# Scores of a differential attention: two stacked products over 128 rows, or three over 64

## The chip, the cores and the metric

The kernel runs on one core of a Trainium2 chip. The metric is the device time of one execution in microseconds, as the median of several runs. The engines are named as in the profile: PE is TensorE's matmuls and PEld its weight loads, DVE is VectorE, ACT is ScalarE, POOL is GpSimd, SP is SyncE, which issues most of the transfers. Line numbers such as L921 are those of the kernel before, unless the text says that they are of the kernel after.

## The reference

The reference is one step of a trunk of two layers over 512 sample tokens and 128 prompt tokens with 1024 features. Each layer projects the normalised tokens once, and three branches read the projection: latent attention, differential attention, and a bidirectional mLSTM. Their gated outputs go through one output projection to the residual. The change touches the differential attention. Per head, with `q_b` and `k_b` of 128 features that hold two maps of 64 features each:

```python
o1 = attention(q_b[..., :DIFF_D], keys_b[..., :DIFF_D], vals_b, DIFF_SCALE)
o2 = attention(q_b[..., DIFF_D:], keys_b[..., DIFF_D:], vals_b, DIFF_SCALE)
o_b = rmsnorm(o1 - lam * o2, W['diff_norm'][l]) * (1.0 - lam_init)
```

A sample token attends to the 512 sample keys and to 128 cached context keys, 640 in all; a prompt token attends to the 128 prompt keys.

## The kernel before

All 640 tokens are worked on in five tiles of 128: four of the sample (`t` 0 to 3) and one of the prompt (`t` 4). Large products keep float32 accuracy by splitting each operand in a high part that the fast matmul takes exactly (float32r) and the rest, the low part: `mm3` (L287 to L290) sends high x high, high x low and low x high. Weights stream in sections through `load_w`: a transfer on SP's queue, the high part by ScalarE (L279), the low part by VectorE or GpSimd (L282). Projections of sections are the `tm` (token-major) and `fm` (feature-major) matmuls; `op` is the output projection.

The order of the work is made in two steps. The program text is a chain of dependent steps (four mLSTM heads, four differential heads, then latent attention), each a generator that yields a number of microseconds; at each yield `Feed.pull` (L107) emits that much independent work from a list (`ORDER`, L133), mostly projections. `feed.need` emits at once what a step needs. Then the framework's scheduler, which simulates the engines, orders the instructions of each engine; the queues themselves run in that order.

Differential attention: `sec_dqk` projects q and k of a head, token-major and rotated. `diff_prep` (L882) transposes them into `pq` and `pkd`, feature-major, with map 0 on rows 0 to 63 and map 1 on rows 64 to 127. `q_stack` (L799) then writes for each map one tile `qs` of 128 rows, its high part above its low part. `k_stack` (L808) writes for each map `ksh` (the high part of the keys, twice) and `ksl` (the low part, twice), and the same for the prompt keys in `kp`. So a score needs two products over 128 rows, `[q_hi; q_lo]` with `[k_hi; k_hi]` and with `[k_lo; k_lo]`, and these hold all four partial products:

```python
T.matmul(pv[:, hf], lhsT=lq, rhs=ks[m][0][:, hf * 320:(hf + 1) * 320], start=True, stop=False)
T.matmul(pv[:, hf], lhsT=lq, rhs=ks[m][1][:, hf * 320:(hf + 1) * 320], start=False, stop=True)
```

These are L921 and L922 (L925 and L926 for the prompt tile); `ds` is their tile in PSUM, one of two buffers of two banks that all transposes of a head share with it. `diff_head` (L900) calls `s1(t)` for the scores of a token tile: for each map the matmuls, a reduction to the maximum (L927), a small scaling (L928) and the exponential (L929); then the two maps are combined into one (L932 to L934). `s2_` transposes the result (`pT`), copies it to `PT` and multiplies by the values (`po`). The preparation of head `h + 1` is called in head `h` before the last `s2_`; that of head 0 stands at the start of head 0.

An mLSTM head (`mlstm_head`, L707) works through five token tiles `c`, each ending with L772 to L777 on VectorE, and closes with a norm and `finish`, whose transposes are `oT`.

Of the kernel before, what the change touches and what calls it, by code (L numbers as in the profile page):

```python
# [9 lines left out]
F32 = mybir.dt.float32  # L10
F32R = mybir.dt.float32r
# [7 lines left out]
P = 128  # L19
# [13 lines left out]
# columns of the constant array  # L33
C_ID, C_SEL, C_BLK, C_ONE, C_PRM, C_RC, C_RS, C_MF, C_END = (
    0, 128, 130, 138, 266, 436, 692, 948, 1204)
# columns of the parameters among them
# [29 lines left out]
def parameter_columns(I):  # L66
    """Vectors of the inputs laid out as columns of 128, and the gate biases and stabilisers on their gate rows."""
    names = ("c", "c_ctx", "g_norm", "mla_q_norm", "mla_kv_norm", "diff_norm", "ml_conv", "ml_norm",
             "state_mlstm_n", "b_mod")
    c = np.zeros((P, C_RC - C_PRM), np.float32)  # L70
    c[:, 0:R_GB] = np.concatenate([I[n].reshape(-1, P) for n in names]).T
    for d in range(2):
        for ty in range(2):
            q0 = ty * 64 + d * 32
            c[q0:q0 + H, R_GB:R_GB + DEPTH] = I["ml_gate_b"][:, d, ty, :].T
        c[d * 32:d * 32 + H, R_M0:R_M0 + DEPTH] = I["state_mlstm_m"][0, :, d, :].T
    return c


class Feed:  # L80
    """Independent work, emitted in portions between the steps of a dependent chain."""
# [41 lines left out]
def tile_hybrid(ctx: ExitStack, tc: tile.TileContext, I: dict, O: dict):  # L123
# [8 lines left out]
    # independent work of a layer, in the order in which it fills the gaps of the dependent chains  # L132
# [7 lines left out]
    class Fixed:  # L140
        """One tile from which all that stays in its place is cut."""
# [14 lines left out]
    class Ring:  # L156
        """Slots used in turn, for tiles that live for a short stretch of the program."""
# [32 lines left out]
    # ---------------------------------------------------------------- constants and parameters  # L190
# [12 lines left out]
    # silu(cond) as stationary columns: [c_hi, ctx_hi, c_lo, ctx_lo] per k  # L203
# [13 lines left out]
    # half conv weights; norm gains with the half of z's silu  # L217
# [29 lines left out]
    # ---------------------------------------------------------------- helpers  # L247
    def rsq(ss, n, mul, eps=EPS):
        """1/sqrt(ss*mul + eps) on [P, n] columns."""
# [13 lines left out]
    def load_w(parts, kt, w, pool=3):  # L263
        """Streams a weight section; returns per-k views of its exact high and low parts."""
# [27 lines left out]
    # ---------------------------------------------------------------- modulation  # L292
# [4 lines left out]
    def mod_rows(l, c0, pool):  # L297
        ps = pj("modp")
        if pool is None:
            # before there is other work for the tensor engine: unsplit  # L300
# [34 lines left out]
    def mod_col(l, part, s, res, pool=3):  # L335
        """Columns [P, k, which] of two feature tiles of the shift or of the scale."""
# [13 lines left out]
    def mod_end(l, res, k=slice(0, 8)):  # L350
        """(1 + scale) * g and shift."""
# [21 lines left out]
    def gate_tile(l, hf):  # L373
        """The residual gates of half of the features for the sample and for the prompt, on all partitions."""
# [5 lines left out]
    # ---------------------------------------------------------------- residual stream  # L380
# [48 lines left out]
    def norm_sample(s, xs, mods, hT):  # L429
        """Two feature tiles of the normalised sample: transposed, modulated and split."""  # L430
# [8 lines left out]
    def norm_prompt(s, xs, mods, hT):  # L439
        """Four feature tiles of the normalised prompt."""  # L440
# [16 lines left out]
    # ---------------------------------------------------------------- projections  # L457
# [9 lines left out]
    def fm_unit(hT, wv, c0, cb):  # L467
        """Feature-major unit of 128 columns: cb(half, psum of 320 tokens)."""
# [9 lines left out]
    def tm_unit(hT, wv, w, cb):  # L478
        """Token-major unit: cb(token tile, psum [P, w])."""
# [8 lines left out]
    def z_sec(l, hT, key, c0, res, h):  # L488
        """2 * silu(z) of a head, feature-major."""
# [10 lines left out]
    def head_norm(tok, sq, mul):  # L500
        """rmsnorm over the 128 features of each of the 5 token tiles; in place."""
# [7 lines left out]
    def finish(tok, tmp, gcol, z):  # L509
        """Token-major head output -> gated, feature-major, split in high and low."""  # L510
# [11 lines left out]
    def out_proj(l, br, ks, res, key, v):  # L522
        """x += gate * (heads ks of a branch) @ W_out, for all tokens."""
# [19 lines left out]
    def out_tail(l, br, ks, res, key, v):  # L543
        """The last heads of a layer, token tile by token tile; gives the new residual tiles."""
# [21 lines left out]
    # ---------------------------------------------------------------- branch C: mLSTM  # L566
    def sec_va(l, hT, p, res):
        """Values of a pair of heads (and the gates with the first pair), token-major."""
# [35 lines left out]
    def conv_unit(l, hT, wv, c0, ch, res, key):  # L604
        """Depthwise conv and silu, feature-major."""
# [15 lines left out]
    def gates(l, res):  # L621
# [42 lines left out]
        # final stabilisers of the prompt  # L664
# [42 lines left out]
    def mlstm_head(l, h, res, feed, nfin):  # L707
# [8 lines left out]
        # value of [C | n] at the start of each chunk  # L716
# [33 lines left out]
        for c in range(NT):  # L750
            if c < 4:
                # q scaled by the weight of the incoming state
# [25 lines left out]
            yield 4.8  # L778
        feed.need(("mo", p), ("zc", h))
# [7 lines left out]
    # ---------------------------------------------------------------- attention pieces  # L787
    def rope(dst, x, t, s, on=None):
        """dst, x: [P, s*64] of sample token tile t."""
# [9 lines left out]
    def q_stack(ps, r0, n):  # L799
        """rows r0..r0+64 of ps -> [q_hi; q_lo], for each of r0."""  # L800
# [7 lines left out]
    def k_stack(ps, parts):  # L808
        """(r0, n0, kh, kl): rows r0..r0+64 of ps from column n0 -> [k_hi; k_hi], [k_lo; k_lo]."""
# [11 lines left out]
    def attend(pe, t, v3, vp, hs):  # L821
        """psum [q, dv] = P @ V, P token-major."""
# [12 lines left out]
    # ---------------------------------------------------------------- branch B: differential attention  # L835
    def sec_dv(l, hT, p, res):
        """Values of a pair of heads: sample | context cache, and prompt."""
# [16 lines left out]
    def sec_dqk(l, hT, h, res):  # L854
        """q | k of a head, token-major, rotated; the context cache as fifth key tile."""
# [25 lines left out]

    def diff_prep(l, h, res):  # L882
        x3, pr, kc = res["dqk", h]
# [3 lines left out]
        qs = q_stack(pq, (0, 64), TOK)  # L887
# [5 lines left out]
        kp = qt("kp", F32R, 512)  # L893
        ks = [(qt("ksh", F32R), qt("ksl", F32R)) for m in range(2)]
        kps = [(kp[:, m * 256:m * 256 + P], kp[:, m * 256 + P:m * 256 + 2 * P]) for m in range(2)]
        k_stack(pk, [(64 * m, n0, *k[m]) for n0, k in ((0, ks), (TOK, kps)) for m in range(2)])
        yield 6.4
        res["dst", h] = (qs, ks, kps)

    def diff_head(l, h, res, feed):  # L900
# [9 lines left out]
        def s1(t):  # L910
            sc = st("dsc")
            pe = []
            n = TOK if t < 4 else P
            for m in range(2):
                lq = qs[m][:, t * P:(t + 1) * P]
                ex = qt("P")
                ps = s2("ds")
                if t < 4:
                    pv, ev, ax = halves(ps), ex.rearrange("p (a n) -> p a n", a=2), AX.XY
                    for hf in range(2):  # L920
                        T.matmul(pv[:, hf], lhsT=lq, rhs=ks[m][0][:, hf * 320:(hf + 1) * 320], start=True, stop=False)  # L921
                        T.matmul(pv[:, hf], lhsT=lq, rhs=ks[m][1][:, hf * 320:(hf + 1) * 320], start=False, stop=True)  # L922
                else:
                    pv, ev, ax = ps[:, 0:P], ex[:, 0:P], AX.X
                    T.matmul(pv, lhsT=lq, rhs=kps[m][0], start=True, stop=False)  # L925
                    T.matmul(pv, lhsT=lq, rhs=kps[m][1], start=False, stop=True)  # L926
                V.tensor_reduce(sc[:, m:m + 1], pv, axis=ax, op=ALU.max, negate=True)  # L927
                V.tensor_scalar(sc[:, 2 + m:3 + m], sc[:, m:m + 1], DIFF_SCALE, None, op0=ALU.mult)  # L928
                A.activation(ev, pv, AF.Exp, scale=DIFF_SCALE, bias=sc[:, 2 + m:3 + m], accum_out=sc[:, 4 + m:5 + m])  # L929
                pe.append(ex[:, 0:n])  # L930
                yield 1.5
            V.reciprocal(sc[:, 6:8], sc[:, 4:6])  # L932
# [432 lines left out]
```

## Time and profile before

| | us |
|---|---|
| median of 3 runs | 1401.21 |
| lowest and highest run | 1399.54, 1405.23 |
| span of the profiled execution | 1399.6 |
| matmuls (PE) busy | 1310.0 |
| VectorE busy | 842.5 |
| ScalarE busy | 630.2 |
| GpSimd busy | 385.5 |

The profiled execution's own time is its span, from the first to the last instruction. Busy times overlap: an engine's share of the span says how much room it has, and the waits of the engine that has none say what else the time is made of. A matmul's row has its start and a modelled end; matmuls overlap in the pipeline, so the cost of one is read from the distance between starts. A wait is written behind an instruction as [idle before <- what it waited for].

### The profile page before, as it was taken

How to read it: one execution, taken by the hardware profiler on the slowest of the kernel's cores; microseconds unless marked ns; L12 is line 12 of the kernel's file. 1: busy time of each engine (PE TensorE's matmuls, PEld its weight loads, DVE VectorE, ACT ScalarE, POOL GpSimd, SP SyncE). 2: the span in 40 equal slices, each digit the busy share in tenths (PEclk: the TensorE clock that was granted, in tenths of full speed). 3: DMA queues.
4: the chain of work that ended last, by engine and by line, in shares of the span. 5: the costliest groups of instructions: out<-in, count | busy, mean ns of one | idle time of the engine just before them, and what ended most of it. 6: DMA issues, size and time to landing. Idle time of an engine off the chain costs nothing.

```text
span 1399.6 us, 24039 instructions
## 1 busy us (share of the span) xinstructions
PE 1310.0 (94%) x9300; PEld 1218.9 (87%) x9300; DVE 842.5 (60%) x1786; ACT 630.2 (45%) x1333; POOL 385.5 (28%) x335
## 2 busy tenths in 40 slices
PE   8989999989899999999979899999999999899995
PEld 3789899969899999798769899998799999878984
DVE  2576757765567465854465767675655646385446
ACT  5454544433455545255365345443343445435433
POOL 0421422323223013511432213333322202161142
PEclk9999999999999999999989999999999999999998
DMA  9423323264223223531751333434521211242154
GB/s 341 116 83 101 111 84 112 85 212 136 81 83 111 61 62 113 167 109 54 238 176 31 84 112 86 117 82 129 180 84 57 74 46 63 87 138 85 54 173 150
DMA packets 164642, 156.40 MB, mean 112 GB/s; under 512 B 14193, under 2 KB 130593, under 8 KB 164529
## 3 DMA queue, kind: packets, MB, share of 16 engines
q1 hardware_dynamic: 154032, 135.92, 32.0%
q10 hardware_dynamic: 10496, 18.95, 3.6%
q8 instruction: 73, 1.20, 0.3%
q14 instruction: 41, 0.33, 0.1%
HBM read 131.38 MB, written 23.46 MB: 111 GB/s over the span
## 4 chain that ended last, share of the span: by engine, by line
PE 73%; DVE 12%; DMA 5%; ACT 4%; issue 2%; POOL 2%; SPq 1%; DVEq 0%; ACTq 0%; POOLq 0%
PE tm L288 8%; PE tm L289 8%; PE tm L290 8%; PE fm L288 6%; PE fm L290 6%; PE fm L289 6%; PE po L831 5%; PE op L288 2%; PE pT L826 2%; PE op L289 2%; PE op L290 2%; DVE fixr L282 1%; PE nd L767 1%; PE ds L921 1%; DVE ksl L816 1%
## 5 line engine op out<-in xcount | busy, mean ns | idle before, releaser
L288 PE MATMUL tm<-fixr 128*128 128x256 f32 (+2 forms) x1040 | 302.0, 291 | 12.4 <-DVE kp L816 4.8
L289 PE MATMUL tm<-fixr 128*128 128x256 f32 (+2 forms) x1040 | 299.4, 288 | 0.2 <-DVE fixr L282 0.2
L290 PE MATMUL tm<-fixr 128*128 128x256 f32 (+2 forms) x1040 | 297.0, 287 | 2.5 <-DVE fixr L427 2.2
L282 POOL TENSOR_TENSOR fixr<-fix,fixr 128x1024 fp32r<-128x1024 f32 (+4 forms) x51 | 121.4, 2380 | 385.0 <-ACT fixr L279 365.4
L279 ACT CAST fixr<-fix 128x1024 fp32r<-128x1024 f32 (+2 forms) x154 | 157.8, 1030 | 128.7 <-PE fm L289 38.4
L288 PEld LDWEIGHTS tm<-fixr 128*128 128x128 f32 x1040 | 201.0, 193 | 15.3 <-issue 4.7
L290 PEld LDWEIGHTS tm<-fixr 128*128 128x128 f32 x1040 | 200.3, 193 | 3.0 <-DVE fixr L427 2.4
L289 PEld LDWEIGHTS tm<-fixr 128*128 128x128 f32 x1040 | 201.0, 193 | 1.4 <-issue 0.9
L288 PE MATMUL fm<-fixr 128*128 128x320 f32 x640 | 201.3, 314 | 0.5 <-ACT od L940 0.5
L290 PE MATMUL fm<-fixr 128*128 128x320 f32 x640 | 199.3, 311 | 0.0
L289 PE MATMUL fm<-fixr 128*128 128x320 f32 x640 | 198.6, 310 | 0.0
L282 DVE TENSOR_TENSOR fixr<-fix,fixr 128x1024 fp32r<-128x1024 f32 (+3 forms) x103 | 141.6, 1377 | 66.8 <-ACT fixr L279 62.3
L288 PEld LDWEIGHTS fm<-fixr 128*128 128x128 f32 x640 | 120.3, 188 | 2.2 <-ACT od L940 0.8
L290 PEld LDWEIGHTS fm<-fixr 128*128 128x128 f32 x640 | 120.2, 188 | 0.9 <-issue 0.9
L289 PEld LDWEIGHTS fm<-fixr 128*128 128x128 f32 x640 | 120.4, 188 | 0.0
L539 POOL TENSOR_TENSOR xp<-xp,ytmp 128x512 f32<-128x512 f32 x60 | 79.1, 1329 | 107.7 <-DVE ytmp L538 58.4
L288 PE MATMUL op<-fixr,oTh 128*128 128x512 f32 x240 | 100.5, 419 | 2.9 <-ACT oTh L516 1.7
L289 PE MATMUL op<-fixr,oTh 128*128 128x512 f32 x240 | 96.7, 403 | 0.0
L290 PE MATMUL op<-fixr,oTl 128*128 128x512 f32 x240 | 95.0, 403 | 0.0
L929 ACT ACTIVATE P<-ds,fix 128x640 f32<-128x640 f32 (+1 forms) x80 | 56.7, 709 | 72.7 <-DVE fix L928 70.4
L927 DVE TENSOR_REDUCE fix<-ds 128x1 f32<-128x640 f32 (+1 forms) x80 | 56.8, 713 | 47.4 <-PE ds L922 31.0
L252 POOL TENSOR_TENSOR fix<-fix 128x5 f32<-128x5 f32 (+1 forms) x31 | 31.6, 1019 | 130.4 <-DVE fix L251 129.9
(325 smaller groups left out, 2722.2 us busy)
## 6 DMA issues: line engine op xcount, KB each, us to landing
fix<-in_W_in SPq DMA_DIRECT2D x56, 512.0 KB, 4.2
fix<-in_W_mod SPq DMA_DIRECT2D x35, 512.0 KB, 4.3
fix<-in_W_in SPq DMA_DIRECT2D x64, 256.0 KB, 3.3
xd<-xp ACTq DMA_DIRECT2D x60, 256.0 KB, 2.5
xp<-xd SPq DMA_DIRECT2D x50, 256.0 KB, 4.4
fix<-in_W_out SPq DMA_DIRECT2D x24, 512.0 KB, 5.0
gate<-grow SPq DMA_DIRECT2D x32, 256.0 KB, 5.0
wm<-in_W_mod SPq DMA_DIRECT2D x26, 256.0 KB, 5.9
```

Of the source, the lines that this page charges most:

```text
L252: G.tensor_tensor(r[:, :n], a[:, :n], mhalf[:, :n], op=ALU.pow)
L279: A.copy(hv, rv)
L282: e.tensor_tensor(lv, rv, hv.bitcast(F32), op=ALU.subtract)
L288: T.matmul(ps, lhsT=wh, rhs=xh, start=start, stop=False)
L289: T.matmul(ps, lhsT=wh, rhs=xl, start=False, stop=False)
L290: T.matmul(ps, lhsT=wl, rhs=xh, start=False, stop=stop)
L539: G.tensor_tensor(xt, xt, y, op=ALU.add)
L767: T.matmul(nd[:, d, 0:129], lhsT=e[:, d], rhs=va[:, c, :], start=True, stop=(c == 4))
L826: T.transpose(ps[:, c * P:(c + 1) * P], pe[:, c * P:(c + 1) * P], idt)
L831: T.matmul(po[:, 0:P], lhsT=pt[:, c * P:(c + 1) * P], rhs=v3[:, c] if t < 4 else vp[:, hs], start=(c == 0), stop=(c == n - 1))
L927: V.tensor_reduce(sc[:, m:m + 1], pv, axis=ax, op=ALU.max, negate=True)
L929: A.activation(ev, pv, AF.Exp, scale=DIFF_SCALE, bias=sc[:, 2 + m:3 + m], accum_out=sc[:, 4 + m:5 + m])
```

## The change

Scores are made of three products (high x high, high x low, low x high) over the 64 rows of a map, and the matmuls of the two maps alternate in the program text: map 0 reads rows 0 to 63 and map 1 rows 64 to 127, each into a score buffer of its own. The stacks go: q, k and the prompt's k are split once each on all 128 rows, by `split2`, one ScalarE and one VectorE instruction. The preparation asks for 3.2 instead of 6.4 us of other work at its second pause. The product low x low is no longer computed. Both score buffers and both `P` tiles are taken at the start of `s1`. The preparation of head 0 is called in the last mLSTM head, after its fourth token tile. Comments are dropped too, which moves line numbers only.

```diff
@@ mlstm_head, at the end of the loop over c
             yield 4.8
+            if c == 3 and h == H - 1:
+                feed.need(("dqk", 0))
+                yield from diff_prep(l, 0, res)
@@ before and in diff_prep
+    def split2(hi, lo, src):
+        A.copy(hi, src)
+        V.tensor_tensor(lo, src, hi.bitcast(F32), op=ALU.subtract)
+        return hi, lo
...
-        qs = q_stack(pq, (0, 64), TOK)
+        qs = split2(qt("qh", F32R), qt("ql", F32R), pq[:, 0:TOK])
         yield 2
...
-        kp = qt("kp", F32R, 512)
-        ks = [(qt("ksh", F32R), qt("ksl", F32R)) for m in range(2)]
-        kps = [(kp[:, m * 256:m * 256 + P], kp[:, m * 256 + P:m * 256 + 2 * P]) for m in range(2)]
-        k_stack(pk, [(64 * m, n0, *k[m]) for n0, k in ((0, ks), (TOK, kps)) for m in range(2)])
-        yield 6.4
+        ks = split2(qt("ksh", F32R), qt("ksl", F32R), pk[:, 0:TOK])
+        kp = qt("kp", F32R, 2 * P)
+        kps = split2(kp[:, 0:P], kp[:, P:2 * P], pk[:, TOK:TOK + P])
+        yield 3.2
@@ diff_head, s1(t)
+            kk = ks if t < 4 else kps
+            pss = [s2("ds") for m in range(2)]
+            exs = [qt("P") for m in range(2)]
...
+            for hf, ck in cols:
+                for i_, (a, b) in enumerate(((0, 0), (0, 1), (1, 0))):
+                    for m in range(2):
+                        rows = slice(64 * m, 64 * m + 64)
+                        T.matmul(pvs[m][:, hf], lhsT=qs[a][rows, t * P:(t + 1) * P], rhs=kk[b][rows, ck],
+                                 start=(i_ == 0), stop=(i_ == 2))
             for m in range(2):
...
-                    for hf in range(2):
-                        T.matmul(pv[:, hf], lhsT=lq, rhs=ks[m][0][:, hf * 320:(hf + 1) * 320], start=True, stop=False)
-                        T.matmul(pv[:, hf], lhsT=lq, rhs=ks[m][1][:, hf * 320:(hf + 1) * 320], start=False, stop=True)
...
-                V.tensor_reduce(sc[:, m:m + 1], pv, axis=ax, op=ALU.max, negate=True)
+                V.tensor_reduce(sc[:, m:m + 1], pvs[m], axis=ax, op=ALU.max, negate=True)
```

What the scheduler makes of it, at two places. The first is TensorE's queue in head 0 of layer 0, at one score tile between other matmuls (`op` is the output projection, `tm` a projection of tokens). Before, one map's scores, both column halves:

```order
L290 MATMUL op<-fixr,oTl 128x512
L921 MATMUL ds<-ksh,qs 128x320
L922 MATMUL ds<-ksl,qs 128x320
L921 MATMUL ds<-ksh,qs 128x320
L922 MATMUL ds<-ksl,qs 128x320
L288 MATMUL op<-fixr,oTh 128x512
```

After the change, in the same head (L935 is the line of all score matmuls there):

```order
L289 MATMUL tm<-fixr 128x256
L935 MATMUL ds<-ksh,qh 128x320
L935 MATMUL ds<-ksl,qh 128x320
L935 MATMUL ds<-ksh,ql 128x320
L935 MATMUL ds<-ksh,qh 128x320
L935 MATMUL ds<-ksl,qh 128x320
L935 MATMUL ds<-ksh,ql 128x320
L290 MATMUL tm<-fixr 128x256
```

Again one map stands alone, three products for each of two column halves; the other map's six matmuls stand in another place, with projections between. In the program text the two maps alternate, so that each product would come twice in a row.

The second place is VectorE's queue around the preparation of head 0 in layer 0. Before, it stands behind the finish of the last mLSTM head (L514) and between the output projection's steps (L538), and the first score reductions (L927) follow:

```order
L514 SCALAR_TENSOR_TENSOR sq<-oT,fix,sz 128x640
L347 TENSOR_TENSOR fix<-mcp,fix 128x4
L805 TENSOR_TENSOR qs<-pq,qs 64x640 x2
L538 TENSOR_TENSOR ytmp<-op,gate 128x512
L816 TENSOR_TENSOR ksl<-pkd,ksh 64x640 x4
L816 TENSOR_TENSOR kp<-pkd,kp 64x128 x4
L538 TENSOR_TENSOR ytmp<-op,gate 128x512 x2
L927 TENSOR_REDUCE fix<-ds 128x1 x2
```

After the change:

```order
L282 TENSOR_TENSOR fixr<-fix,fixr 128x1024 x2
L887 TENSOR_TENSOR ql<-pq,qh 128x640
L887 TENSOR_TENSOR ksl<-pkd,ksh 128x640
L347 TENSOR_TENSOR fix<-mcp,fix 128x4
L772 SCALAR_TENSOR_TENSOR fix<-nd,fix 128x2
L773 TENSOR_TENSOR fix<-nd,fix 128x2
L774 RECIPROCAL fix<-fix 128x2
L776 TENSOR_SCALAR hs<-nd,fix 128x128
L887 TENSOR_TENSOR kp<-pkd,kp 128x128
L777 SCALAR_TENSOR_TENSOR hs<-nd,fix,hs 128x128
```

The preparation now stands ahead of the last token tile of the mLSTM head (L772 to L777), in three instructions where there were ten.

## Rows read from the trace of the kernel before

**Rows 1.** The page: busy time of each engine and its share.

```profile
PE 1310.0 (94%) x9300; PEld 1218.9 (87%) x9300; DVE 842.5 (60%) x1786; ACT 630.2 (45%) x1333; POOL 385.5 (28%) x335
```

**Rows 2.** TensorE's waits, 280 to 470 us (layer 0): total us, times, longest.

```profile
PE ds L922 <- DVE ksl L816: 3.9, 1, 3.9
PE tm L288 <- DVE sz L496: 3.0, 1, 3.0
PE ds L921 <- DVE kp L816: 2.3, 1, 2.3
PE tm L288 <- DVE kp L816: 1.5, 1, 1.5
```

**Rows 3.** The same waits from 960 to 1215 us, layer 1.

```profile
PE tm L288 <- DVE kp L816: 3.3, 2, 2.5
PE ds L921 <- DVE kp L816: 2.2, 1, 2.2
PE ds L922 <- DVE ksl L816: 2.0, 1, 2.0
```

**Rows 4.** Windows: length, engines' busy us, then PEclk, DMA share and GB/s.

```profile
280.00:302.00 22.00, 15.78 (x68) 12.63 (x67) 12.43 (x22) 8.61 (x16) 7.76 (x5) 0.84 0.66 215
360.00:376.00 16.00, 11.26 (x67) 10.59 (x66) 11.61 (x18) 6.93 (x14) 3.52 (x2) 0.79 0.44 140
...
974.00:990.00 16.00, 11.76 (x45) 9.21 (x44) 9.59 (x18) 4.85 (x12) 4.22 (x4) 0.79 0.51 164
```

**Rows 5.** Timeline of TensorE, a score tile: first matmul, and the one behind the fourth.

```profile
304.02 0.31 PE L921 MATMUL ds<-ksh,qs 128*128 128x320 f32 x1
...
304.61 0.39 PE L288 MATMUL op<-fixr,oTh 128*128 128x512 f32 x1
```

**Rows 6.** Instructions on the tile `ds`: ns shortest, median, longest; first and last start.

```profile
L921 PE MATMUL ds<-ksh,qs x128: 302/310/605, 288.4 to 1197.5; 128*128 128x320 f32 x128
...
L927 DVE TENSOR_REDUCE fix<-ds x80: 280/815/826, 296.8 to 1207.1; 128x1 f32<-128x640 f32 x64, 128x1 f32<-128x128 f32 x16
L929 ACT ACTIVATE P<-ds,fix x80: 360/794/812, 298.4 to 1207.6; 128x640 f32<-128x640 f32 x64, 128x128 f32<-128x128 f32 x16
```

**Rows 7.** Timeline of TensorE around two matmuls on 4 rows.

```profile
167.08 0.28 PE L288 MATMUL tm<-fixr 128*128 128x256 f32 x1
167.29 0.59 PE L367 MATMUL gtp<-fix 4*2 4x256 f32 x2
167.81 0.39 PE L289 MATMUL tm<-fixr 128*128 128x256 f32 x1
168.03 0.28 PE L290 MATMUL tm<-fixr 128*128 128x256 f32 x1
```

**Rows 8.** Instructions on the tile `gtp`, as in rows 6.

```profile
L367 PE MATMUL gtp<-fix x16: 372/373/374, 136.1 to 949.1; 4*2 4x256 f32 x16
```

**Rows 9.** Timeline of TensorE around matmuls and transposes on 64 rows.

```profile
99.05 0.28 PE L289 MATMUL tm<-fixr 128*128 128x256 f32 x1
99.26 0.45 PE L690 MATMUL abp<-fix 64*128 64x80 f32 x2
99.55 0.47 PE L697 MATMUL pb<-fix,gtb 64*128 64x64 f32 x5
99.94 0.39 PE L290 MATMUL tm<-fixr 128*128 128x256 f32 x1
100.16 0.28 PE L288 MATMUL tm<-fixr 128*128 128x256 f32 x1
100.28 0.28 PE L289 MATMUL tm<-fixr 128*128 128x256 f32 x1
```

**Rows 10.** Instructions on the tile `pq`: the low part of q.

```profile
L805 DVE TENSOR_TENSOR qs<-pq,qs x16: 817/824/830, 284.1 to 1157.8; 64x640 fp32r<-64x640 f32 x16
```

**Rows 11.** Instructions on the tile `pkd`: the low parts of k.

```profile
L816 DVE TENSOR_TENSOR ksl<-pkd,ksh x32: 816/822/828, 291.0 to 1163.4; 64x640 fp32r<-64x640 f32 x32
L816 DVE TENSOR_TENSOR kp<-pkd,kp x32: 282/289/295, 294.3 to 1165.1; 64x128 fp32r<-64x128 f32 x32
```

More of the change, by code (lines that the diff above doesn't have):

```diff
@@ L911, in s1 @@
             sc = st("dsc")
-            pe = []
             n = TOK if t < 4 else P
-            for m in range(2):
[L915 to L919, printed above, removed]
-                    for hf in range(2):
-                        T.matmul(pv[:, hf], lhsT=lq, rhs=ks[m][0][:, hf * 320:(hf + 1) * 320], start=True, stop=False)
-                        T.matmul(pv[:, hf], lhsT=lq, rhs=ks[m][1][:, hf * 320:(hf + 1) * 320], start=False, stop=True)
[L923 to L926, printed above, removed]
-                V.tensor_reduce(sc[:, m:m + 1], pv, axis=ax, op=ALU.max, negate=True)
+            kk = ks if t < 4 else kps
@@ new lines, in s1 @@
+            pss = [s2("ds") for m in range(2)]
+            exs = [qt("P") for m in range(2)]
+            if t < 4:
+                pvs, evs, ax = [halves(x) for x in pss], [x.rearrange("p (a n) -> p a n", a=2) for x in exs], AX.XY
+                cols = [(hf, slice(hf * 320, (hf + 1) * 320)) for hf in range(2)]
+            else:
+                pvs, evs, ax = [x[:, 0:P].unsqueeze(1) for x in pss], [x[:, 0:P].unsqueeze(1) for x in exs], AX.XY
+                cols = [(0, slice(0, P))]
+            for hf, ck in cols:
[4 more added lines that the diff above has]
+                                 start=(i_ == 0), stop=(i_ == 2))
@@ L928, in s1 @@
+            for m in range(2):
+                V.tensor_reduce(sc[:, m:m + 1], pvs[m], axis=ax, op=ALU.max, negate=True)
                 V.tensor_scalar(sc[:, 2 + m:3 + m], sc[:, m:m + 1], DIFF_SCALE, None, op0=ALU.mult)
-                A.activation(ev, pv, AF.Exp, scale=DIFF_SCALE, bias=sc[:, 2 + m:3 + m], accum_out=sc[:, 4 + m:5 + m])
-                pe.append(ex[:, 0:n])
+                A.activation(evs[m], pvs[m], AF.Exp, scale=DIFF_SCALE, bias=sc[:, 2 + m:3 + m],
+                             accum_out=sc[:, 4 + m:5 + m])
@@ L931, in s1 @@
                 yield 1.5
+            pe = [x[:, 0:n] for x in exs]
             V.reciprocal(sc[:, 6:8], sc[:, 4:6])
```

## The prediction

> **What bounds the kernel now.** I read the busy shares first, then what TensorE waits for in the two stretches where differential attention runs, then its timeline. TensorE's matmuls are busy 94% of the span, VectorE 60% and ScalarE 45% [rows 1], so a microsecond more of matmul is a microsecond more of time wherever TensorE does not wait. In the stretch of layer 0 it waits for four things worth naming: 3.9 and 2.3 us for the low halves of the keys of head 0, 3.0 us for a VectorE step (`sz`) that stands behind the key work of head 1, and 1.5 us for the same work of a later head [rows 2]. In layer 1 the same kinds come to 3.3, 2.2 and 2.0 us [rows 3]. All are waits for the preparation of a head: 10.7 + 7.5 = 18.2 us. After the long ones the clock is granted at half speed for a while: the mean granted clock is 0.84 over 22 us, 0.79 over 16 and 0.79 over 16 around them [rows 4], that is (1 - 0.84) x 22 + 2 x (1 - 0.79) x 16 = 10.2 us lost. So preparation costs TensorE at most some 28 us in 1400, and matmuls of the scores are the other thing that the change touches.
>
> **The change part by part.** My sum is against the profiled execution, whose span is 1399.6 us; the median of the three runs, 1401.2, lies 1.6 above it.
>
> *More matmuls, and no pairs.* A score tile of 320 columns is sent every (304.61 - 304.02) / 4 = 0.147 us [rows 5]. Before, a sample tile takes two products x two column halves x two maps = 8 of them, 4 tiles x 8 heads x 8 = 256, which is the 128 of L921 [rows 6] and as many of L922. Now it takes three products: 12. If the two maps ran side by side in the two row halves, 12 would cost the time of 6. But the order that the scheduler writes does not keep the two maps next to each other: the code alternates them, and so each product would stand twice in a row; in the order shown each stands once, six matmuls of one map, then projection work, then six of the other map. Over the program there are 68 such stretches, and in only a dozen places does a matmul of one map directly follow one of the other. Matmuls in the same row half cannot overlap each other's columns, so I price each at 0.147: 32 tiles x 4 more x 0.147 = +18.8 us. The prompt tile has 6 instead of 4 of 128 columns; by columns (an estimate, 0.147 x 128 / 320 = 0.059) that is 8 x 2 x 0.059 = +0.9. Together **+19.7 us**.
>
> *Leaving the 128-row shape.* The score matmuls now contract 64 rows. The trace of before has matmuls on fewer rows, and each excursion costs TensorE time around it. The projection matmuls of 256 columns start 0.12 us apart (100.16 to 100.28 [rows 9]). Two `gtp` matmuls on 4 rows stand between two of them [rows 7]: the projection matmul ahead lasts 167.29 - 167.08 = 0.21, 0.09 too long; the pair of `gtp`, whose second starts 0.59 - 0.373 = 0.215 after the first [rows 7, 8] and so should take 0.43, takes 0.52, 0.09 too long; the projection matmul behind takes 0.22, 0.10 too long. That is 0.28 lost. On exactly 64 rows stand `abp` and `pb`: the projection matmul ahead of them takes 99.26 - 99.05 = 0.21 and the one behind 100.16 - 99.94 = 0.22 [rows 9], the same losses of 0.09 and 0.10. Ends: 0, if matmuls of the scores' type leave and enter free (`gtp`, `abp` and `pb` are of other types), and 0.35, if the first matmul inside is slow as well (99.26 to 99.55 for two `abp` [rows 9]). I take 0.28: 68 x 0.28 = **+19.0 us**. [...]
>
> *Less preparation.* Per head VectorE had two q steps of 0.824 [rows 10], four key steps of 0.822 and four of 0.289 [rows 11], each on 64 rows; now it has one of each on all 128 rows. That 128 rows take no longer is seen in the reduction of 128 x 640 from the same memory, 0.815 [rows 6]. So VectorE saves 0.824 + 3 x 0.822 + 3 x 0.289 = 4.16 us a head, and ScalarE as many steps. Both engines have room [rows 1]; this shows in the time only where TensorE waits for it. Head 0's two waits in each layer (3.9 + 2.3 + 2.2 + 2.0 = 10.4 us) go in full, for its preparation now comes before the last token tile of the last mLSTM head, and their slow clock with them (3.5 + 3.4 = 6.9). The waits of later heads (3.0, 1.5 and 3.3) are each shorter than the 4.16 us that VectorE gains; with the slow clock at 360 (3.4) they come to 11.2, and I count 8, since projection work behind them still needs VectorE. **-25.3 us**; ends: 17.3 (head 0 alone) and 28.4.
>
> *Moved past.* In the mLSTM head the two subtractions, 1.6 us, now stand on VectorE ahead of the last tile's normalisation, and that head's transposes for its finish come later; 24 projection matmuls, 24 x 0.12 = 2.9 us, stand ahead of them on TensorE and cover it. Without them it would cost those 1.6 us in each layer. The weights of W_out are fetched later on SP's queue, behind seven loads of W_mod and W_in, and nothing of the preparation runs on POOL; no transfer is among TensorE's waits in these stretches [rows 2, 3], so nothing is put down. The pauses of the preparation ask for 3.2 us less other work per head; TensorE is full there, so that only moves work behind.
>
> *A new wait.* Three heads of layer 0 now begin with 24 score matmuls in a row, two token tiles. The second tile needs the score buffers of the first, and there are two. From the end of a map's matmuls the reduction (0.815) and the exponential (0.794) [rows 6] have to pass, 1.6 us, with small steps and handovers some 2.5 (an estimate); the other map's six matmuls cover 6 x 0.147 = 0.9. So about 1.6 us each, three times: **+4.8 us**, ends 0 and 10.
>
> Sum: 19.7 + 19.0 - 25.3 + 4.8 = +18.2, so 1399.6 + 18.2 = **1418 us**. What a measurement of this kernel can tell from no change is about 0.5%, 7 us.
>
> **Rivals.**
> 1. *Waits pay for the matmuls* (about the same). If an excursion costs only the two changes of shape (0.09 in, 0.09 out, 0.18 in all), and every wait goes: 19.7 + 12.2 - 28.4 = +3.5, 1403 us. For it: each wait is smaller than the relief. Against: both excursions read lose 0.28.
> 2. *Free excursions* (faster). The lossy excursions in the trace are of other types than the scores; if score matmuls enter and leave the 64-row shape free and all waits go, 19.7 - 28.4 = -8.7, 1391 us. It decides below 0.13 us per excursion, where 19.7 + 68 x 0.13 meets 28.4. Against: the loss stands on the projection matmul ahead too, which is of the scores' type.
> 3. *Weight loads in the open* (slower still). If inside one row half the next weights can't be loaded under the running matmul, each of the 432 pays for its load. Five `pb` on 64 rows, each with a load of its own, take 99.94 - 99.55 = 0.39, of which 0.09 is the way out [rows 7, 9]: 0.06 each. So a load takes at most 0.06, and 432 x 0.06 = +26 gives 1444 us. The same rows speak against it: 64 columns and a load fit into 0.06 together. [...]
> 4. *The halves run side by side after all*, as the change says: six slots a tile for eight, -32 x 2 x 0.147 = -9.4 in place of +18.8, 1418 - 28 = 1390 us. The order leaves it almost no place.
>
> **Chances.** Forecast 0.59, rivals 0.20, 0.10, 0.08 and 0.03. The forecast's own range: with waits back to 17.3 and the new wait at 10, 19.7 + 19.0 - 17.3 + 10 = +31, 1431; with an excursion of 0.35 also 1436; at the other end with no new wait and all waits gone, +10, 1410. With rival 1 inside, 1400 to 1436 leaves out rivals 2 to 4. Faster: rival 2 and most of 4, 0.12. Same: rival 1 and a little of the forecast's low end, 0.22. Slower: 0.66.
>
> **What the next profile would show.** Right: score matmuls 432 in number, 0.147 apart, with the projection matmul ahead of each stretch at 0.2 and the one behind also late; no wait of a score matmul for key low halves; the granted clock near 1 where it was 0.84 and 0.79. Waits inside runs of 24. Wrong: score matmuls starting in pairs a few ns apart; starts 0.2 apart inside a stretch (rival 3); projection matmuls that run on undisturbed next to a stretch (rival 2); or waits of another kind, such as projections for their buffers, in the places of the old ones.

## The result and the profile after

The changed kernel takes 1435.6 us (median of 4 runs, 1431.8 to 1442.7) against 1400.9 for the kernel before beside it: a ratio of 1.0242, 95% interval 1.0208 to 1.0277. It is 34.7 us slower; the forecast was 17 us slower, with a range up to 1436. The profiled execution has a span of 1436.8 us. From here on line numbers are those of the kernel after, which the experiments share unless they add lines. The page's busy times, to be read against [rows 1]:

```profile
PE 1354.5 (94%) x9444; PEld 1246.1 (87%) x9444; DVE 799.9 (56%) x1730; ACT 603.3 (42%) x1277; POOL 386.5 (27%) x335
```

VectorE and ScalarE did become lighter, by 43 and 27 us, and TensorE's matmuls are busy 44 us longer, with 144 instructions more. TensorE's waits in the two stretches of [rows 2, 3], layer 0 first (280 to 470 us):

```profile
PE ds L935 <- ACT P L940: 2.1, 2, 1.0
PE oT L513 <- DVE hs L507: 2.1, 1, 2.1
PE pT L829 <- DVE fix L939: 1.8, 1, 1.8
...
PE op L288 <- DVE ytmp L538: 1.7, 1, 1.7
PE tm L288 <- DVE fix L799: 1.7, 1, 1.7
PE ds L935 <- ACT P L940: 1.4, 1, 1.4
```

The last three are layer 1, 960 to 1215 us. No wait for the halves of keys is left. But others stand there: score matmuls and transposes wait for the exponential (L940) and the small scaling ahead of it (L939), and in layer 0 the finish of the last mLSTM head waits 2.1. Together 6.0 and 4.8, where all waits of before came to 14.1 and 7.7, 10.7 and 7.5 of it for the preparation. The windows, with the granted clock as the third figure from the end, as in [rows 4], and then the two whole stretches of differential attention:

```profile
280.00:302.00 22.00, 19.95 (x143) 18.34 (x141) 16.93 (x30) 7.76 (x13) 8.18 (x5) 1.00 0.56 168
360.00:376.00 16.00, 13.15 (x76) 12.05 (x76) 10.17 (x21) 7.51 (x14) 5.42 (x4) 0.80 0.50 160
...
490.00:506.00 16.00, 14.96 (x97) 14.10 (x96) 10.21 (x20) 6.27 (x17) 2.71 (x2) 0.79 0.10 34
...
295.40:532.90 237.50, 232.58 (x1630) 213.34 (x1629) 115.34 (x247) 92.77 (x194) 53.74 (x38) 0.96 0.31 92
1002.70:1231.90 229.20, 224.38 (x1546) 206.32 (x1545) 112.24 (x236) 86.79 (x187) 46.73 (x33) 0.96 0.26 79
```

Head 0's slow clock is gone, but the one at 360 is as it was, and there are new ones. (1 - 0.96) of 237.5 and 229.2 us is 18.7 us, by these rounded figures the most that the clock takes in these stretches.

The price of the shape is read from one stretch of six score matmuls in TensorE's timeline:

```profile
305.98 0.28 PE L289 MATMUL tm<-fixr 128*128 128x256 f32 x1
306.19 0.41 PE L935 MATMUL ds<-ksh,qh 64*128 64x320 f32 x1
306.44 0.31 PE L935 MATMUL ds<-ksl,qh 64*128 64x320 f32 x1
306.59 0.30 PE L935 MATMUL ds<-ksh,ql 64*128 64x320 f32 x1
...
307.02 0.30 PE L935 MATMUL ds<-ksh,ql 64*128 64x320 f32 x1
307.26 0.38 PE L290 MATMUL tm<-fixr 128*128 128x256 f32 x1
307.48 0.28 PE L288 MATMUL tm<-fixr 128*128 128x256 f32 x1
307.60 0.28 PE L289 MATMUL tm<-fixr 128*128 128x256 f32 x1
```

Inside, the distance is 0.15, and from the third on each load of weights starts with the matmul ahead of its own (at 306.44 for the one at 306.59), so the next weights are loaded under the running matmul although all six stand in one row half. But the projection ahead takes 0.21 instead of 0.12, the first score matmul 0.25 instead of 0.147, the last 0.24, and the first projection behind 0.22. The stretch, counted from the start of the projection ahead to that of the third behind, less three projections of 0.12, takes 1.27 us (the median of 47 such stretches); six times 0.147 would be 0.88.

### The profile page after: what moved, and what is told of

It reads as the page before. It is cut to its first block, busy times and chain, and to the rows that moved or that the text cites. A ratio compares the mean times of both kernels' runs of the same rounds, so it can differ in the third digit from the quotient of the medians.

```text
span 1436.8 us, 24196 instructions
## 1 busy us (share of the span) xinstructions
PE 1354.5 (94%) x9444; PEld 1246.1 (87%) x9444; DVE 799.9 (56%) x1730; ACT 603.3 (42%) x1277; POOL 386.5 (27%) x335
## 4 chain that ended last, share of the span: by engine, by line
PE 80%; DVE 8%; ACT 3%; DMA 3%; POOL 2%; issue 2%; SPq 0%; ACTq 0%; DVEq 0%; POOLq 0%
PE tm L288 8%; PE tm L290 8%; PE tm L289 8%; PE fm L288 6%; PE fm L290 6%; PE fm L289 6%; PE po L834 5%; PE ds L935 5%; PE op L288 3%; PE op L289 3%; PE op L290 3%; PE pT L829 2%; PE nd L767 1%; PE modp L320 1%; PE as L1161 1%
## 5 line engine op out<-in xcount | busy, mean ns | idle before, releaser
L288 PE MATMUL tm<-fixr 128*128 128x256 f32 (+2 forms) x1040 | 305.7, 294 | 5.6 <-ACT va L581 2.4
L290 PE MATMUL tm<-fixr 128*128 128x256 f32 (+2 forms) x1040 | 300.3, 290 | 2.9 <-DVE fixr L427 2.2
L289 PE MATMUL tm<-fixr 128*128 128x256 f32 (+2 forms) x1040 | 301.9, 291 | 0.2 <-DVE fixr L282 0.2
L940 ACT ACTIVATE P<-ds,fix 128x640 f32<-128x640 f32 (+1 forms) x80 | 56.8, 710 | 88.6 <-DVE fix L939 82.9
L252 POOL TENSOR_TENSOR fix<-fix 128x5 f32<-128x5 f32 (+1 forms) x31 | 32.7, 1056 | 146.3 <-DVE fix L251 146.0
```

The source lines that it names most:

```text
L252: G.tensor_tensor(r[:, :n], a[:, :n], mhalf[:, :n], op=ALU.pow)
L288: T.matmul(ps, lhsT=wh, rhs=xh, start=start, stop=False)
L289: T.matmul(ps, lhsT=wh, rhs=xl, start=False, stop=False)
L290: T.matmul(ps, lhsT=wl, rhs=xh, start=False, stop=stop)
L940: A.activation(evs[m], pvs[m], AF.Exp, scale=DIFF_SCALE, bias=sc[:, 2 + m:3 + m], accum_out=sc[:, 4 + m:5 + m])
```

## The experiments

Three kernels take the change apart: its shape, its third product, its preparation. Their score stretches are summed from TensorE's timeline in the way just told. The difference is the median less that of the kernel before in the same comparison; its 95% interval is 2.5 to 5 us either way, and that of a difference between two of these rows 3.5 to 6.

| kernel | score matmuls | difference, us | score stretches in all, us |
|---|---|---|---|
| before | 2 products, 128 rows | 0 | 57.7 |
| lighter, earlier preparation | 2 products, 128 rows | -8.8 | 62.5 |
| the same | 3 products, 128 rows | +2.0 | 73.7 |
| the same | 2 products, 64 rows | +17.7 | 86.1 |
| the changed kernel | 3 products, 64 rows | +34.7 | 99.1 |

The sums hold the waits of more than 0.15 us that stand in a stretch or right behind it: 11.8, 15.0, 7.9, 12.4 and 9.7 us, from the top of the table to its end.

**The shape alone.** The changed kernel with 128 rows in each score matmul:

```diff
-                        rows = slice(64 * m, 64 * m + 64)
+                        rows = slice(0, P)
```

> The changed kernel with its score matmuls contracting all 128 rows: the same 432 matmuls in the same order, but the array's shape never changes for them (both maps then give the scores of the whole 128 rows, so the computation is changed). Theory A (an excursion into the 64-row shape costs about 0.375 us, as the trace of the changed kernel shows around its stretches): 68 x 0.375 = 25 us come back, less the few that a wait would have covered, so about 1411 us, 20 to 28 below the changed kernel, and the projection matmuls beside the score stretches start 0.12 apart again. Theory B (the dear places are the third product and waits, and the shape costs at most 0.1): 1429 or more. Theory C (as in my forecast, 0.28): 1417.

It took 1404.2 us, 1.0013 of the kernel before (0.9994 to 1.0032). The same stretch in its timeline:

```profile
300.58 0.28 PE L289 MATMUL tm<-fixr 128*128 128x256 f32 x1
300.70 0.31 PE L935 MATMUL ds<-ksh,qh 128*128 128x320 f32 x1
300.85 0.31 PE L935 MATMUL ds<-ksl,qh 128*128 128x320 f32 x1
...
301.43 0.31 PE L935 MATMUL ds<-ksh,ql 128*128 128x320 f32 x1
301.58 0.28 PE L290 MATMUL tm<-fixr 128*128 128x256 f32 x1
301.70 0.28 PE L288 MATMUL tm<-fixr 128*128 128x256 f32 x1
```

Nothing around it is late: 0.88 for six. The shape costs 1.27 - 0.88 = 0.39 a stretch, and for the prompt tile's three 0.67 against 0.34. Over all stretches that is 99.1 - 73.7 = 25.4 us, as Theory A had it. In time it is 34.7 - 2.0 = 32.7 us, give or take 5.5: above the 25 of Theory A, though not clear of its upper end, 28. The windows of the two attention stretches of this run show what else differs:

```profile
297.00:516.20 219.20, 214.76 (x1613) 203.87 (x1612) 114.88 (x248) 91.85 (x194) 53.82 (x38) 1.00 0.33 99
990.00:1199.40 209.40, 205.30 (x1548) 198.17 (x1546) 112.61 (x236) 86.16 (x187) 46.72 (x34) 1.00 0.28 85
```

The granted clock is 1.00 in both, where it was 0.96 on 64 rows, although the same long runs of scores with the same kind of wait stand there. Over the two spans the clock, 0.975 of 1436.8 us against 0.982 of 1403.9, takes some 10 us more at most on 64 rows. That the remaining 7 us are clock is what these rows suggest; no run holds the clock alone.

**Two products.** The third one left out, on 128 rows and on 64:

```diff
-                for i_, (a, b) in enumerate(((0, 0), (0, 1), (1, 0))):
+                for i_, (a, b) in enumerate(((0, 0), (0, 1))):
...
-                                 start=(i_ == 0), stop=(i_ == 2))
+                                 start=(i_ == 0), stop=(i_ == 1))
```

> The changed kernel with its scores as two products over all 128 rows (the third product left out and the rows of both maps summed, so the computation is changed): the number and shape of the score matmuls of the kernel before, with the lighter and earlier preparation of the changed one. Theory A (TensorE is full, each of the 144 matmuls of the third product costs its 0.147 or 0.11 in full, and the lighter preparation is worth some 17 us): 20 us below the run with three products on 128 rows, that is 1382 to 1388 us, 14 to 20 below the kernel before. Rival (the preparation gains little by itself, and with fewer matmuls TensorE waits longer for the exponentials): 1393 to 1402.

> The changed kernel without its third product (query low halves against key high halves left out, so the scores are less exact): 64 rows kept, 288 score matmuls in about as many stretches. Theory A (count and excursions are separate prices, 20 us and 25 to 31 us): 1436 - 20 = 1416 us, and 25 to 31 above the same two products on 128 rows. Rival (the excursion cost is partly the third product's own, as a wait for the low half of the query): stretches lose less than 0.3 us each, and the two kernels of two products lie within 15 us.

They took 1394.4 (0.9945, 0.9927 to 0.9963) and 1421.0 (1.0123, 1.0096 to 1.0150). So the shape costs 26.5 us with two products, 0.976 - 0.588 = 0.39 in each stretch of four: it is the shape's and not the third product's. The third product itself costs 10.8 us on 128 rows, where the rival came, and 17.0 on 64, where Theory A's time was 5 too low; the intervals do not tell 10.8 from 17.0, nor 26.5 from 32.7. Its matmuls add 32 x 4 x 0.147 and 16 x 0.11, that is 20.6 us, but on 128 rows the stretches grow only from 62.5 to 73.7: without the waits they grow by 18.3, and the waits in them fall from 15.0 to 7.9. The waits that are left in layer 0 of the run with two products on 128 rows, 262 to 490 us, show why:

```profile
PE ds L935 <- ACT P L940: 3.2, 3, 1.1
PE tm L288 <- DVE fix L799: 2.1, 1, 2.1
PE oT L513 <- DVE hs L507: 2.0, 1, 2.0
```

The heads that begin with two token tiles in a row wait for the exponential; one map's matmuls are the cover, and six cover more than four: on 128 rows the score matmuls' waits for it in layer 0 are 3.2 us with two products and 2.0 with three.

**The move.** Head 0's preparation at its old place, in the changed kernel and in the run with two products on 128 rows; and the move by itself in the kernel before:

```diff
-            if c == 3 and h == H - 1:
-                feed.need(("dqk", 0))
-                yield from diff_prep(l, 0, res)
```

> The changed kernel without the earlier preparation of head 0: the scores on 64 rows alone. Theory A (the move takes away the waits for head 0, 10.4 us and their slow clock 6.9, a little less because head 0 now has lighter preparation anyway): 10 to 17 us slower than the changed kernel, 1446 to 1453 us, with TensorE waiting again in both layers for the low halves of q and of k. Rival (the lighter preparation alone had removed the waits, or waits of another kind stand in their place): within 4 us of the changed kernel.

> Two products over 128 rows with the lighter preparation (computation changed as in the run with two products on 128 rows, which took 1394), and head 0 prepared at its old place. Theory A (the move is worth 11.5 us beside lighter preparation, as it was on 64 rows): 1406 us, so lighter preparation alone gains nothing against the kernel before, and the move alone gained nothing either; only both together give 9 us. Rival (the 11.5 us were tied to the 64-row kernel, and lighter preparation alone brings the 9 us): 1393 to 1397.

> The kernel before with the earlier preparation of head 0 alone, stacks on 128 rows and two products kept. Theory A (the move is worth the waits of head 0 and their slow clock): 10 to 17 us faster than before, 1384 to 1391 us, faster than both kernels. Rival (other waits take the place of those, for instance the finish of the last mLSTM head behind ten steps of preparation on VectorE, 6.6 us in this heavier form): within 5 us of the kernel before, 1396 to 1406.

Without the move the changed kernel took 1447.2 us (1.0309, 1.0281 to 1.0336), two products on 128 rows 1398.6 (0.9968, 0.9955 to 0.9981); the kernel before with the move alone 1401.6 (0.9997, 0.9982 to 1.0011). The move is worth 10 us on 64 rows, 5 beside light preparation on 128 rows (between that run's two expectations), and nothing with the heavy one. On 64 rows Theory A's time came, but not its waits: without the move one wait for key halves stands there,

```profile
PE ds L932 <- ACT ksh L883: 1.0, 1, 1.0
```

and TensorE's waits come to some 68 us over the whole run with the move and without it. What differs is the number of score stretches, 75 against 68 (7 x 0.39 = 2.7 us), and the mean granted clock, 0.972 against 0.975 (some 5 us at most); which of these the move acts through was not tested. Where its gain went with the heavy preparation the waits of that run tell (the whole run):

```profile
PE op L288 <- DVE ytmp L538: 4.1, 3, 3.1
PE tm L288 <- DVE kp L819: 3.5, 1, 3.5
PE ds L924 <- ACT P L932: 3.2, 4, 1.2
```

Head 0's waits are gone, yet all of TensorE's waits together only go from 75 to 74 us. Projections wait for key halves as before (3.5 and 1.4 here, L819 in that kernel; 4.8 before), and 4.1 for the output projection's step on VectorE and 3.2 of score matmuls for exponentials are new (0.2 and none before). Neither half of the preparation's change brings what both together bring, 8.8 us: the lighter form alone gives 3.9, the move alone nothing that can be told.

**The pairs.** The maps forced to alternate on TensorE, by an order without waits between each score matmul and the next:

```diff
-                    for m in range(2):
+                    for m in (1, 0):
...
+                        if prev is not None:
+                            tc.add_manual_dep(mm.ins, prev.ins.name, mybir.DependencyInfo(
+                                mybir.DependencyClass.NoSync, mybir.DependencyReason.DATA), reason="alternate")
+                        prev = mm
```

> The changed kernel with its score matmuls held in the order map 1, map 0, map 1, map 0 on TensorE; the first of each tile still goes ahead alone, so there are 65 stretches on 64 rows, against 68. The computation is the same. Theory A (the two row halves do run side by side on the chip, and only the order kept them from it): 11 of 12 matmuls of a tile stand in alternation, about 6.5 slots of 0.147 for 12, so 32 x 5.5 x 0.147 = 26 us less, 1410 us, with starts of a few ns and of 0.147 in turn. Rival (matmuls of two row halves take turns on the chip): starts stay 0.147 apart and the time within 5 us of the changed kernel, 1436. Half-way rival (they overlap, but each weight load stands in the open between them): about 0.1 apart, 1420.

It took 1451.3 us (1.0364, 1.0322 to 1.0406), 14 more than the changed kernel instead of 26 less. Yet the pairs are there. TensorE's timeline (x2 is a pair):

```profile
305.12 0.28 PE L290 MATMUL tm<-fixr 128*128 128x256 f32 x1
305.33 0.42 PE L936 MATMUL ds<-ksh,qh 64*128 64x320 f32 x2
305.59 0.30 PE L936 MATMUL ds<-ksl,qh 64*128 64x320 f32 x2
305.73 0.32 PE L936 MATMUL ds<-ksh,ql 64*128 64x320 f32 x2
...
306.04 0.31 PE L936 MATMUL ds<-ksl,qh 64*128 64x320 f32 x2
306.18 0.31 PE L936 MATMUL ds<-ksh,ql 64*128 64x320 f32 x2
309.29 0.77 PE L829 MATMUL pT<-fix,P 128*128 128x128 f32 x5 [2.80 <-ACT P L945]
```

Twelve matmuls in six slots; the two of a pair start within 0.01 us of each other (the first pair's row takes 0.42 us, the first matmul of a one-map stretch 0.41). Then comes a wait of 2.8. The waits of that run:

```profile
PE pT L829 <- ACT P L945: 20.6, 8, 2.9
PE ds L936 <- ACT P L945: 16.7, 6, 3.4
```

37 us of waits for exponentials. With both maps in one run, both score buffers are taken at once, and the transposes of the tile before, which need one, stand right behind. The control has the same forced order on all 128 rows, without half-height matmuls:

> The control to the first alternating run: the same forced order of the score matmuls, but each contracting all 128 rows, so that nothing can run side by side and the shape never changes (the computation is changed as in the run with three products on 128 rows and the maps apart, which took 1404). Theory A (the forced order itself costs about 37 us of waits for exponentials, because both score buffers are taken and given back together, and what pairing saves in matmuls is smaller than that): 30 to 40 above 1404, that is 1434 to 1444 us, with 30 us or more of waits for exponentials. Rival (the waits came from the pairs' being sooner done, or the order costs nothing): 1404 to 1415.

```profile
PE pT L829 <- ACT P L945: 19.6, 8, 2.7
PE ds L936 <- ACT P L945: 16.9, 7, 3.3
```

It took 1461.5 us (1.0416, 1.0391 to 1.0441), 56 more than the maps apart on 128 rows, with 36.5 us of the same waits against 37.3: the loss is the order's and not the pairs'. The waits are Theory A's, the time is 17 us above its range. For the other 20 us of the 56 the clock is at hand: 0.970 of 1459.1 us against 0.982 of 1403.9 is some 18.5 us at most, and it is 0.95 in both attention stretches there; no run holds it alone. On 64 rows the same order takes some 9 us less, so pairing is worth more than the shape costs, but not what its order costs.

A tile's two pauses at 3.0 us in place of 1.5, to put other work ahead of the transposes, with the maps alternating and, as a control, apart:

```diff
                              accum_out=sc[:, 4 + m:5 + m])
-                yield 1.5
+                yield 3.0
```

> The alternating order of the maps again, with the two pauses behind a tile's scores drawn at 3.0 us of other work in place of 1.5, so that projection matmuls stand between a tile's scores and the transposes that wait for its exponentials. The computation is the same. Theory A (eleven matmuls in pairs cost 1.27 us, as six of one map did, and the loss of the first alternating run lay in 37 us of waits for exponentials, because both score buffers are taken and given back together): with the waits gone 1436 - 26 = 1410, within 1403 to 1416. Rival (the waits return wherever the other work is put, since a tile's chain of reduction, exponential, transposes and copy is longer than the time between tiles): 1425 or more, with over 20 us of waits for exponentials.

> The control to that run: the changed kernel as it is, its maps apart, with the same longer pauses of 3.0 us. If the pauses by themselves change little (Theory A), 1428 to 1438 us, at best the 4 to 5 us of waits inside the runs of 24 less. Rival (the pauses are what moves the time, and the pairing nothing): as far below the changed kernel as the alternating run with the same pauses.

They took 1465.2 us (1.0445, 1.043 to 1.0461) and 1463.9 (1.0435, 1.0379 to 1.0492). Theory A missed in both. With the maps alternating the rival's figures came, more than 1425 us and more than 20 of waits for exponentials. Of the control's rival one half holds: the pauses move the time and the pairing does not, but upwards. The longer pauses cost 26 us with the maps apart, and the alternating order is no dearer than that. Waits of the one with the maps apart, and then of the alternating one:

```profile
PE oT L513 <- DVE od L507: 10.7, 3, 4.5
```

```profile
PE pT L829 <- ACT P L945: 19.5, 9, 2.8
PE tm L288 <- ACT P L945: 5.2, 2, 2.7
```

The projections that fill the pauses are used up sooner, and the finish of a head (`oT`) then waits with nothing beside it: 10.7 us in both runs, where the changed kernel has no such wait. That is less than half of the 26; the rest was not traced. The waits of the pairs for exponentials fell from 37.3 to 24.7, and the time rose all the same. A pairing order that does not wait was not found.

**A wait that the sum did not have.** In both layers TensorE waits for the shared rotary key, whose last step is POOL's; in layer 0, 570 to 620 us:

```profile
PE krT L1067 <- POOL krr L800: 4.6, 1, 4.6
```

Before, it was 1.3. That step on VectorE:

```diff
-        G.tensor_tensor(dst, dst, tmp[:, 0:s * 64], op=ALU.add)
+        (on or G).tensor_tensor(dst, dst, tmp[:, 0:s * 64], op=ALU.add)
...
-            rope(kx[:, t], kr3[:, t], t, 1)
+            rope(kx[:, t], kr3[:, t], t, 1, on=V)
```

> The changed kernel with the last addition of the shared rotary key (64 columns, four of them a layer) on VectorE instead of on POOL. The computation is the same. Theory A (TensorE's wait of 4.6 us for that addition, which on POOL stands behind two additions of the residual, is a cost of the changed kernel that my sum did not have): 3 to 6 us less, 1430 to 1433 us, with that wait gone. Rival (what comes next in that stretch, the rotary queries or the residual's own loads, is as late): within 2 us of 1436.

1435.2 us (1.0235, 1.0213 to 1.0256), no difference that can be told from the changed kernel. The wait of 4.6 went, and others came in the same stretch:

```profile
PE pqr L1089 <- POOL qrt L800: 2.3, 1, 2.3
PE uv L288 <- DVE ytmp L538: 1.4, 1, 1.4
```

**A version meant to beat both.** Stacks and two products on 128 rows, the move, and POOL to copy each key half once more instead of ScalarE and VectorE making it twice:

```diff
-            for a in (0, 64):
-                A.copy(kh[a:a + 64], x)
+            A.copy(kh[0:64], x)
...
+                G.tensor_copy(kh[64:128], kh[0:64])
+                G.tensor_copy(kl[64:128], kl[0:64])
```

> A version meant to be faster than both: the kernel before with its stacks and two products on 128 rows, head 0 prepared in the last mLSTM head, and the second copy of each key half made by POOL from the first, so that ScalarE and VectorE do half of the key steps (2.2 us a head less on each). The computation is the same. Theory A (the preparation on VectorE and ScalarE is what held the move back, since move and lighter preparation gained 9 us together): 1394 to 1399 us, 2 to 8 below the kernel before. Rival (POOL's copies come late in its in-order queue, or hold up what POOL has to do for the projections): 1402 or more, with waits of score matmuls for POOL.

1405.0 us (1.0016, 1.0007 to 1.0026): not faster. Score matmuls do not wait for POOL; they and the transposes wait for exponentials:

```profile
PE ds L933 <- ACT P L941: 5.9, 7, 1.2
...
PE pT L838 <- ACT P L941: 4.6, 5, 1.6
```

No kernel here that computes the scores in full is faster than the kernel before.

## Why the prediction was right, and where it was off

The direction and its two causes were right: more score matmuls without pairs, and the way out of the 128-row shape, are dearer than what the preparation gives back. The time stands at the upper end of the range, because three terms were mis-sized, and not all to the same side. That it still lies inside, by 0.4 us, is luck: two of the errors are larger than 10 us, and the third took 9 back.

- **More matmuls**, +19.7: the count holds (0.147 apart in stretches of one map; the prompt's at 0.11 instead of 0.059, 20.6 in all). In time the third product cost 10.8 us on 128 rows and 17.0 on 64, because its matmuls also cover waits for the exponential (15.0 us in the stretches with two products on 128 rows, 7.9 with three). The step that failed is the full distance as the price of each: it holds, as the prediction itself says, only where TensorE does not wait, and inside a run of scores it waits.
- **Leaving the shape**, +19.0: 0.28 per excursion, taken from the matmuls on 4 rows; measured are 0.39 for six and 0.34 for the prompt's three. The first score matmul inside is slow as well (0.25), which was the upper end, 0.35, that I set aside. That makes 25.4 us in the stretches, and 32.7 in time by the run on 128 rows.
- **Less preparation**, -25.3, and **the new wait**, +4.8: together -20.5 forecast, -8.8 measured, in the run with two products on 128 rows. The waits for key halves went as said, in both layers, and the clock of head 0 with them. But in the changed kernel 10.8 us of other waits stand in the same stretches, which had 21.8; slow clock turned up in other places (0.79 at 490); and 7.5 us of waits in the two layers are for the rotary key, of which the 4.6 of layer 0 went to 0.4 without a gain, so that waits are not simply added. The new wait alone came to 6.9 us: the three runs of 24 take 7.8, 5.6 and 5.3 against 24 x 0.147 + 0.39 = 3.9 each.
- **Moved past**, nothing: the cover of 2.9 us did not hold in layer 0, where `oT` waits 2.1 for the last mLSTM head, about the 1.6 that I named for that case. In layer 1 no such wait shows.
- The three errors against the measured pieces: preparation 12 too large, third product 9 too dear, shape 14 too cheap; 18.2 + 11.7 - 8.9 + 13.7 = 34.7. They add up because each kernel of the table is one step from the next; by the other path, the shape first, the third product (17.0) is 2.7 too dear and the shape (26.5) 7.5 too cheap, and the intervals do not decide between the two.

Of the rivals, "free excursions" and "waits pay" fall with the 0.39. Weight loads are hidden in one row half (0.15 apart), so "weight loads in the open" falls as well, and `pb` spoke against it already [rows 9]. "The halves run side by side" is true of the chip (the two of a pair start within 0.01 us) and was rightly put down to the order: by hand it can be had, at a price higher than its gain. Even without a wait it would not have won on matmuls: six slots and one excursion are 0.88 + 0.39 = 1.27 us a tile (eleven in pairs measure 1.27, the quickest twelve 1.36), against 2 x 0.588 = 1.18 for the two stretches of four before.

## What to carry to other kernels

Count what a narrower matmul does to its neighbours, not only its own slots: a stretch of six on half the rows cost 0.39 us more than on all rows, and with 68 of them the 8.8 us that the lighter and earlier preparation gives were paid about three times over. Two half-height matmuls of different row halves shared a slot of 0.147 us where they stood next to each other in TensorE's queue, while in stretches of one map each took a slot of its own; the order that put them together here also tied their buffers together; look at what then waits for these before counting the gain. A wait removed from a full queue can be worth little by itself, when the next late engine stands right behind it: here the lighter preparation brought 3.9 us and the move nothing that can be told, where both together brought 8.8.

## What the runs showed of the hardware that was not expected

The granted clock of the two attention stretches was 1.00 with three products on 128 rows and 0.96 on 64, with the same instructions in about the same order. The shape alone does not decide it: with two products the two stretches have 0.97 and 1.00 on 128 rows,

```profile
294.80:515.30 220.50, 211.06 (x1551) 199.72 (x1550) 117.54 (x247) 91.81 (x193) 55.33 (x38) 0.97 0.32 99
```

and 0.98 and 0.93 on 64 (the second of these two),

```profile
987.80:1217.60 229.80, 222.72 (x1477) 203.71 (x1476) 110.11 (x236) 86.56 (x187) 48.26 (x33) 0.93 0.25 79
```

and the forced order has 0.95 on 128 rows. In the first run of 24 on 64 rows TensorE waits 1.05 us for an exponential, up to 367.70; from 369.43 on its score matmuls are 0.21 apart instead of 0.147, and the granted clock has fallen from 1.00 to 0.50, where it stays through a wait of 1.8 us and 4.3 us of full work, up to 376.20. Windows of 4 us:

```profile
364.00:368.00 4.00, 2.95 (x19) 2.37 (x18) 2.84 (x5) 2.76 (x5) 2.09 (x1) 1.00 0.55 196
368.00:372.00 4.00, 2.20 (x13) 1.70 (x12) 3.01 (x8) 2.30 (x7) 1.78 (x2) 0.69 0.57 178
372.00:376.00 4.00, 4.00 (x20) 4.00 (x21) 1.89 (x5) 1.50 (x3) 0.00 (x0) 0.50 0.01 2
376.00:380.00 4.00, 4.00 (x26) 3.40 (x25) 0.98 (x2) 0.93 (x2) 0.00 (x0) 0.96 0.00 0
```

On 128 rows the same run, 7.3 us long against 7.8 and with waits of 0.87 and 1.80 us at the same places, leaves the clock at 1.00 (the window of 297.00 to 516.20); why was not found. And the two row halves change places at no cost from one matmul to the next (eleven that alternate take 1.27 us, as six of one half do), while a change between half and whole rows costs 0.39 us each time there and back.
